# A four-block decoder trunk on one core: the slabs of the down and output projections in halves at the input blocks' place, another order of passes in the products, rotary products on VectorE

## The chip, the cores and the metric

One Trainium2 chip, one of its cores. The metric is the device time of one execution of the whole program in microseconds, as the median of several runs. Before the change three runs took 1076.57, 1079.47 and 1082.0 us; the median is 1079.47 us.

## The reference, cut to what matters

One sequence of 512 tokens, width 1024, all in float32. Two layers, each a token mixer and a feed-forward part with a convolution, both with a root-mean-square norm ahead and a residual behind:

```python
for layer in range(2):
    if layer == 0:
        h = h + short_conv_mixer(rms_norm(h, g), w_in, conv, w_out)   # 1024 -> 3072, conv, gate, -> 1024
    else:
        h = h + mla_attention(rms_norm(h, g), ..., k_nope, v, k_rope) # 8 heads, causal, rotary part of 64
    h = h + conv_ffn(rms_norm(h, g), w_up, conv, w_down)              # 1024 -> 2 x 2816, conv, silu(g) * u, -> 1024
    if layer == 0:
        k_nope, v, k_rope = shared_latent_kv(h, ...)
return rms_norm(h, final_norm)
```

The rotary part of a query is `[x1*cos - x2*sin, x1*sin + x2*cos]`.

## The kernel before

Everything stands transposed in the on-chip memory: features on the 128 partitions, the 512 tokens along the row. A float32 number is split into a rounded high part and a low part (`whi`, `wlo` for weights, names ending in H and L for activations), and a product of two such numbers is three matmul passes: high by high, high by low, low by high. Each matmul loads its own 128x128 weights.

**Weights** come as chunks of eight 128x128 blocks (512 KB) over the SP queue. `Weights.split` (L202, L203) makes the high part on ScalarE and the low part on VectorE. Four chunks are kept ahead.

**Two widths of matmul.** `gemm` (L330) adds up slabs of activations by `mm3` (L311). A slab that is a tuple of three (`halves`, made by `slab`, L429, and by `hg` in `ffn`) is taken in two halves of 256 tokens, six matmuls (L321 to L323); any other slab is taken in three matmuls of 512 (L325 to L327). The up projection runs mostly as seven products of half-size blocks (`product`, L437; a fast scheme with seven products for eight; P1, P2, P6, P5, P7, P4, P3 in that order), 24 matmuls of 256 each (L447 to L449: high by high, high weights by low activations, low weights by high activations). The input blocks of these, `x`, lie in a pool that starts with `pad(xp, 192)` and ends with `pad(xp, 320)` (`start_x`).

**The order of a feed-forward part** is the list `FFN` (L29): two plain column pairs ("p": two gemms of eight slabs, 48 matmuls of 256 each), then column pairs by products ("Q"). From the second "Q" on, four slices of the down projection ("D": `step`, four gemms over the four hidden slabs of a part, 48 matmuls of 512) stand between P7 and P4 of a "Q"; so from one D to the next run P4, P3 and the next pair's P1, P2, P6, P5, P7: seven products, 168 matmuls of 256. There are eight D of this kind in each layer, the last two of them of two slices (24 matmuls). Then follow "p" for columns 20 and 21, the rest of part 3, and the last part ("E"): in layer 0 as gemms, in layer 1 in `down1` (L955), where the weights stream and 128 columns of the hidden slab are the stationary operand. In layer 1 two groups of 16 transposes of `h` ("R") stand between.

The hidden slabs are made in `two` (L533) by `split` (L340), and those of the mixer's output in `gate` (L675), as pairs of 512-wide tiles; they lie where the allocator puts them, in pools on the right side that are that end at a fixed address, in tiles of 2 KB and 4 KB. All weight tiles lie a multiple of 512 bytes from them. The blocks `x` lie 192 bytes past such a multiple, by their pad.

**Norms.** `Norm.sums` multiplies a matrix of ones with the sums of squares (two matmuls of 512, L374 and L375), VectorE makes the diagonals `nd` (L398), and `Norm.spread` (L405) multiplies ones with them (two matmuls of 512). Their tiles `sq` lie in the pool `ap_`, which starts with `pad(ap_, 160)`; they are 320 bytes past a multiple of 512 from the weights (adding up the tiles of the pools). Most of these calls stand in the middle of a gemm; there are six norms of this form.

**Attention** follows the list `ORDER` (L48): v values, r rope, p project, s scores, a attend, t turn (transposes of the softmax), w output. Its start is v0, v1, r0, p0, p1, s0, r1, p2, t0, s1, a0, p3, t1. The framework that builds the program orders each engine's instructions by a plan of its own, so that neighbouring steps may interleave. PSUM has eight banks; `bank()` hands out two groups of four in turn, so the bank of an allocation is that of the eighth before it. In `rope` (L843) two of six products run on GpSimd (L848, L851), four operations on VectorE (L849, L850, L852, L853).

Of the kernel before, what the change touches and what calls it, by code (L numbers as in the profile page):

```python
# [16 lines left out]
P = 128  # L17
# [29 lines left out]

ORDER = [("v", 0), ("v", 1), ("r", 0), ("p", 0), ("p", 1)]  # L48
for _h in range(NH):
    ORDER += [("s", _h)] + ([] if _h else [("r", 1)]) + ([("a", _h - 1)] if _h else [])  # L50
    if _h < 6:
        ORDER += [("p", _h + 2)]
    elif _h == 6:
        ORDER += [("w", 1, 4, 8)]
    else:
        ORDER += [("w", 2, 4, 6)]
    ORDER += [("t", _h)]
    ORDER += {3: [("w", 0, 0, 4)], 4: [("w", 0, 4, 8)], 5: [("w", 1, 0, 4)], 6: [("w", 2, 0, 4)],
              7: [("w", 2, 6, 8)]}.get(_h, [])
ORDER += [("a", 7), ("w", 3, 0, 8)]  # L60
# [201 lines left out]
def trunk(ctx: ExitStack, tc: tile.TileContext, xT, wst, pvec, tabs, sign, gfin, out):  # L262
# [32 lines left out]

    W = Weights(nc, wp, wst)
    pad(ctx.enter_context(tc.tile_pool(name="rp", bufs=1, side="right")), 32)
    pad(ap_, 160)
    sg = ap_.tile([P, 1], F32, name="sg")
    ss = [ap_.tile([P, 8], F32, name=f"ss{tb}") for tb in range(4)]  # L300

# [40 lines left out]
    def split(pool, tag, bufs, src, gain=None):  # L342
# [7 lines left out]
            V.scalar_tensor_tensor(lo, src, gain, hi, op0=ALU.mult, op1=ALU.subtract)  # L350
        return hi, lo

    class Norm:


# [13 lines left out]
        def sums(self, tag=None):  # L369
            hi, lo = (ap_.tile([P, T], F32R, tag="sq", name=nm("na"), bufs=2) for _ in range(2))  # L370
            S.activation(hi, self.acc, AF.Copy)
            V.tensor_tensor(lo, self.acc, hi, op=ALU.subtract)
            ps = bank(tag)
            PE.matmul(ps, ones, hi, start=True, stop=False)  # L374
            PE.matmul(ps, ones, lo, start=False, stop=True)  # L375

            c = ap_.tile([P, 16], F32, tag="nc", name=nm("nc"), bufs=2)
            d = ap_.tile([P, T], F32, tag="sq", name=nm("nd"), bufs=2)
            for b in range(4):
                bs = slice(b * P, b * P + P)  # L380
                V.tensor_tensor_reduce(out=d[:, bs], in0=ps[:, bs], in1=ident, scale=1.0, scalar=0.0,
                                       op0=ALU.mult, op1=ALU.add, accum_out=c[:, b:b + 1])
            v, t, r, e = (c[:, 4 * i:4 * i + 4] for i in range(4))
            V.tensor_scalar(v, v, 1.0 / (self.n * P), EPS, op0=ALU.mult, op1=ALU.add)
            S.activation(t, v, AF.Sqrt)
            V.reciprocal(r, t)
            V.tensor_tensor(t, v, r, op=ALU.mult)
            V.tensor_tensor(t, t, r, op=ALU.mult)
            V.tensor_scalar(t, t, -0.5, 1.5, op0=ALU.mult, op1=ALU.add)
            V.tensor_tensor(r, r, t, op=ALU.mult)  # L390
            rh = ap_.tile([P, 4], F32R, tag="nh", name=nm("nh"), bufs=2)
            S.activation(rh, r, AF.Copy)
            V.tensor_tensor(e, r, rh, op=ALU.subtract)
            self.d, self.r = [], ap_.tile([P, T], F32, tag="rstd", name=nm("rstd"), bufs=2)
            for x in (rh.bitcast(F32), e):
                d = ap_.tile([P, T], F32R, tag="sq", name=nm("nd"), bufs=2)
                for b in range(4):
                    V.tensor_scalar(d[:, b * P:b * P + P], ident, x[:, b:b + 1], None, op0=ALU.mult)  # L398
                self.d.append(d)

        def spread(self, tag=None):

            ps = bank(tag)
            for i, d in enumerate(self.d):
                PE.matmul(ps, ones, d, start=i == 0, stop=i == 1)  # L405
            S.activation(self.r, ps, AF.Copy)

    def conv(pool, tag, src, c, step, bufs=2):
# [27 lines left out]
    def product(p, x, a):  # L436
# [5 lines left out]
        for i in range(KD // 2):  # L442
            ah, al = (t[:, xb * Q:xb * Q + Q] for t in x[i])
            for s in range(2):
                w = slice((s * KD // 2 + i) * P, (s * KD // 2 + i) * P + P)
                o, z = ps[:, s * Q:s * Q + Q], i == KD // 2 - 1
                PE.matmul(o, wh[:, w], ah, start=begins and i == 0 and s == 0, stop=False, skip_group_check=True)  # L447
                PE.matmul(o, wh[:, w], al, start=False, stop=False, skip_group_check=True)  # L448
                PE.matmul(o, wl[:, w], ah, start=False, stop=z, skip_group_check=True)  # L449

    class Out:

# [55 lines left out]
    def ffn(fp, layer, x, rstd, last, late=()):  # L508
# [9 lines left out]
        def tail(j, g, u):  # L518
# [14 lines left out]
            def two():  # L533
                o = conv1(u, 1)
                V.tensor_tensor(o, o, cell[0], op=ALU.mult)
                hid[j] = split(fp, "hid", HID, o)

            cell = []
            pend.extend([one, two])
# [135 lines left out]
    def gate(m, ps, cc):  # L675
        V.tensor_tensor(ps, ps, rstd, op=ALU.mult)
        V.tensor_tensor(ps, ps, cc, op=ALU.mult)
        ys[m] = split(fpp[1], "hid", KD, ps)

    def mix(m, pc, ph, pb):  # L680
        t = room()
# [8 lines left out]
            mm3(ps, W.take(), hg[k], k == 0, k == KD - 1)  # L690
    for k in range(KD):
        norm.add(h[k])
    pss.append([gemm(hg, norm.sums)])
    for i in range(2):
        xsums(x, i, G_MIX, room)
# [74 lines left out]
    if True:  # L770
# [72 lines left out]
        def rope(half):  # L843
# [1 line left out]
            pa, pb = gemm(ql), gemm(ql, None if half else normq.spread)  # L845
            a, b = (scaled(at, "tm", ps, normq.r, 5) for ps in (pa, pb))
            t, u = (at.tile([P, T], F32, tag="tm", name=nm("rp"), bufs=5) for _ in range(2))
            G.tensor_tensor(u, b, sin, op=ALU.mult)  # L848
            V.tensor_tensor(t, a, cos, op=ALU.mult)  # L849
            V.tensor_tensor(a, a, sin, op=ALU.mult)  # L850
            G.tensor_tensor(b, b, cos, op=ALU.mult)  # L851
            V.tensor_tensor(t, t, u, op=ALU.subtract)  # L852
            V.tensor_tensor(a, a, b, op=ALU.add)  # L853
            s1, s2 = split(ao[1], "o", 4, t), split(ao[1], "o", 4, a)
# [81 lines left out]
    if True:  # L936
# [21 lines left out]
        def down1(part, half, hid):  # L958
# [8 lines left out]

            def step(tb, k, i):
                a, z = cuts[tb][i]
                (wh, wl), (ah, al) = (x[:, a:z] for x in ws[k]), (x[:, tb * P:tb * P + P] for x in hid[ks[k]])  # L970
                o = ps[tb][i][:, :z - a]
                PE.matmul(o, ah, wh, start=k == 0, stop=False)  # L972
                PE.matmul(o, ah, wl, start=False, stop=False)  # L973
# [114 lines left out]
```

## Time and profile before

| | us |
|---|---|
| median of three runs | 1079.47 |
| lowest and highest run | 1076.57, 1082.0 |
| the profiled execution | 1076.78 |
| its span, first to last instruction | 1075.0 |
| PE (TensorE matmuls) busy | 1059.3 |
| DVE (VectorE) busy | 919.5 |
| ACT (ScalarE) busy | 561.5 |
| POOL (GpSimd) busy | 46.4 |

The profiled execution is one of its own, 0.2 us above the lowest of the three runs and 2.7 us under their median; 1.8 us of its time lie outside its span. A matmul's duration in the profile (280 ns for 256 columns, 389 ns for 512) has its pipeline in it; successive matmuls overlap, so the time that one costs is read from the starts of successive matmuls in the timeline, over a stretch of known count.

### The profile page before, as it was taken

The numbers are of one execution on the slowest core, as the hardware profiler recorded it, in microseconds if no ns is written. First come the engines' busy times: TensorE is split into PE (matmuls) and PEld (weight loads), VectorE is DVE, ScalarE is ACT, GpSimd is POOL, SyncE is SP. The second block draws the span as 40 slices with busy tenths as digits, with TensorE's granted clock in tenths as the row PEclk, the third lists the DMA queues.
The fourth block names the chain that finished last, engine by engine and source line by source line (L and its number), as shares of the span: only waits on it lengthen the run. The fifth ranks groups of instructions, "written<-read, shape, count | busy, mean of one in ns | idle before, by whom it ended". The sixth has DMA issues, their size and how long they took to land. (4 is left out here: it accounts for less than half of the span.)

```text
span 1075.0 us, 17920 instructions
## 1 busy us (share of the span) xinstructions
PE 1059.3 (99%) x7178; PEld 979.1 (91%) x7178; DVE 919.5 (86%) x1457; ACT 561.5 (52%) x820; POOL 46.4 (4%) x55
## 2 busy tenths in 40 slices
PE   8999999999999999999999899999999999999997
PEld 8999988999999999998887788889999999999986
DVE  7897878799988899986789887899988889989846
ACT  7544455555444455544655554376644445555444
POOL 0000000000000000000001100000000000000000
PEclk9999999999999999999999999999999999999999
DMA  8455433455555465333332412223545545453422
GB/s 269 130 147 141 113 105 109 133 144 141 134 152 124 131 158 137 79 86 97 124 108 82 116 58 60 75 82 119 157 121 153 122 135 157 126 141 72 135 59 79
DMA packets 38115, 129.25 MB, mean 120 GB/s; under 512 B 4752, under 2 KB 5008, under 8 KB 38032
## 3 DMA queue, kind: packets, MB, share of 16 engines
q1 hardware_dynamic: 32240, 107.14, 31.9%
q0 software_dynamic: 5792, 20.98, 11.4%
q8 instruction: 56, 0.92, 0.4%
q14 instruction: 27, 0.22, 0.1%
HBM read 102.67 MB, written 2.10 MB: 97 GB/s over the span
## 5 line engine op out<-in xcount | busy, mean ns | idle before, releaser
L447 PE MATMUL ps<-xH,whi 128*128 128x256 f32 x1120 | 313.6, 280 | 1.4 <-ACT xs L463 1.3
L448 PE MATMUL ps<-xL,whi 128*128 128x256 f32 x1120 | 313.4, 280 | 0.0
L449 PE MATMUL ps<-xH,wlo 128*128 128x256 f32 x1120 | 313.1, 280 | 0.0
L202 ACT ACTIVATE whi<-wraw 128x1024 fp32r<-128x1024 f32 (+1 forms) x130 | 136.5, 1050 | 158.1 <-issue 57.6
L449 PEld LDWEIGHTS ps<-xH,wlo 128*128 128x128 f32 x1120 | 213.8, 191 | 0.0
L447 PEld LDWEIGHTS ps<-xH,whi 128*128 128x128 f32 x1120 | 210.2, 188 | 2.5 <-ACT xs L463 1.5
L448 PEld LDWEIGHTS ps<-xL,whi 128*128 128x128 f32 x1120 | 210.2, 188 | 0.7
L203 DVE TENSOR_TENSOR wlo<-wraw,whi 128x1024 fp32r<-128x1024 f32 (+1 forms) x130 | 158.5, 1219 | 26.9 <-ACT whi L202 26.3
L321 PE MATMUL ps<-xH,whi 128*128 128x256 f32 x512 | 143.4, 281 | 0.5 <-ACT sg L530 0.5
L322 PE MATMUL ps<-xL,whi 128*128 128x256 f32 x512 | 143.2, 280 | 0.0
L326 PE MATMUL ps<-hidL,whi 128*128 128x512 f32 x368 | 143.1, 389 | 0.0
L323 PE MATMUL ps<-xH,wlo 128*128 128x256 f32 x512 | 143.1, 280 | 0.0
L327 PE MATMUL ps<-hidH,wlo 128*128 128x512 f32 x368 | 143.1, 389 | 0.0
L325 PE MATMUL ps<-hidH,whi 128*128 128x512 f32 x368 | 141.9, 389 | 0.0
L202 ACT ACTIVATE whi<-x 128x1024 fp32r<-128x1024 f32 x60 | 63.6, 1060 | 116.5 <-PE ps L326 51.0
L321 PEld LDWEIGHTS ps<-xH,whi 128*128 128x128 f32 x512 | 97.0, 190 | 1.1 <-ACT sg L530 0.7
L323 PEld LDWEIGHTS ps<-xH,wlo 128*128 128x128 f32 x512 | 97.9, 191 | 0.0
L322 PEld LDWEIGHTS ps<-xL,whi 128*128 128x128 f32 x512 | 97.1, 190 | 0.3
L202 ACT ACTIVATE whi<-xs 128x1024 fp32r<-128x1024 f32 x60 | 63.4, 1057 | 64.2 <-PE ps L448 47.1
L327 PEld LDWEIGHTS ps<-hidH,wlo 128*128 128x128 f32 x368 | 69.1, 188 | 14.3
L326 PEld LDWEIGHTS ps<-hidL,whi 128*128 128x128 f32 x368 | 69.1, 188 | 14.2 <-DVE hidL L347 0.2
L325 PEld LDWEIGHTS ps<-hidH,whi 128*128 128x128 f32 x368 | 68.9, 188 | 14.1 <-ACT hidH L346 0.5
(216 smaller groups left out, 1837.7 us busy)
## 6 DMA issues: line engine op xcount, KB each, us to landing
wraw<-wst SPq DMA_DIRECT2D x128, 512.0 KB, 3.7
x<-wst SPq DMA_DIRECT2D x60, 512.0 KB, 4.4
x<-x POOLq DMA_DIRECT2D x20, 512.0 KB, 5.4
xs<-x POOLq DMA_DIRECT2D x20, 512.0 KB, 4.6
h<-xT SPq DMA_DIRECT2D x8, 256.0 KB, 6.2
out<-r SPq DMA_DIRECT2D x8, 256.0 KB, 2.0
qr<-oH SPq DMA_DIRECT2D x16, 64.0 KB, 2.0
qr<-oL SPq DMA_DIRECT2D x16, 64.0 KB, 2.0
```

What stands on the lines that cost most here:

```text
L202: self.nc.scalar.activation(hi, raw, AF.Copy)
L203: self.nc.vector.tensor_tensor(lo, raw, hi, op=ALU.subtract)
L321: PE.matmul(o, wh, p, start=start and b == 0, stop=False, skip_group_check=True)
L322: PE.matmul(o, wh, q, start=False, stop=False, skip_group_check=True)
L323: PE.matmul(o, wl, p, start=False, stop=stop, skip_group_check=True)
L325: PE.matmul(ps, wh, ah, start=start, stop=False)
L326: PE.matmul(ps, wh, al, start=False, stop=False)
L327: PE.matmul(ps, wl, ah, start=False, stop=stop)
L447: PE.matmul(o, wh[:, w], ah, start=begins and i == 0 and s == 0, stop=False, skip_group_check=True)
L448: PE.matmul(o, wh[:, w], al, start=False, stop=False, skip_group_check=True)
L449: PE.matmul(o, wl[:, w], ah, start=False, stop=z, skip_group_check=True)
```

## The change

- The hidden slabs of both feed-forward parts and the mixer's output slabs are marked as halves, so that `mm3` takes them in six matmuls of 256. Their pools get a pad of 320 bytes behind them, which moves the pool's start, and these slabs, down by 320 bytes: that is 192 bytes past a multiple of 512 from the weights, as `x` is.
- The norm's ones-products are made in halves too (`spread2`), and the pad in front of `ap_` shrinks by 128 bytes, with 128 put in behind the `sq` tiles: these then lie 192 bytes past a multiple of 512 from the weights as well.
- `product` takes the low weights second and the low activations third.
- In `rope` the two products on GpSimd go to VectorE.
- In `ORDER` t0 stands ahead of p2 instead of behind it.
- `down1` takes the first two of a hidden slab's three entries; it is as it was otherwise.

```diff
 for _h in range(NH):
-    ORDER += [("s", _h)] + ([] if _h else [("r", 1)]) + ([("a", _h - 1)] if _h else [])
+    ORDER += [("s", _h)] + ([("a", _h - 1)] if _h else [("r", 1), ("t", 0)])
...
-    ORDER += [("t", _h)]
+    ORDER += [("t", _h)] if _h else []
...
-    pad(ap_, 160)
+    pad(ap_, 32)
...
+    def spread2(ps, parts):
+        for b in range(2):
+            for i, d in enumerate(parts):
+                o, d = (t[:, b * Q:b * Q + Q] for t in (ps, d))
+                PE.matmul(o, ones, d, start=i == 0 and b == 0, stop=i == 1, skip_group_check=True)
+
+    padded = []
+
+    def hidden(pool, n, src):
+
+        o = split(pool, "hid", n, src)
+        if pool not in padded:
+            padded.append(pool)
+            pad(pool, 320)
+        return *o, True
...
-            PE.matmul(ps, ones, hi, start=True, stop=False)
-            PE.matmul(ps, ones, lo, start=False, stop=True)
+            spread2(ps, (hi, lo))
...
-            for i, d in enumerate(self.d):
-                PE.matmul(ps, ones, d, start=i == 0, stop=i == 1)
+            spread2(ps, self.d)
...
-                PE.matmul(o, wh[:, w], al, start=False, stop=False, skip_group_check=True)
-                PE.matmul(o, wl[:, w], ah, start=False, stop=z, skip_group_check=True)
+                PE.matmul(o, wl[:, w], ah, start=False, stop=False, skip_group_check=True)
+                PE.matmul(o, wh[:, w], al, start=False, stop=z, skip_group_check=True)
...
-                hid[j] = split(fp, "hid", HID, o)
+                hid[j] = hidden(fp, HID, o)
...
-        ys[m] = split(fpp[1], "hid", KD, ps)
+        ys[m] = hidden(fpp[1], KD, ps)
...
+    pad(ap_, 128)
     pss.append([gemm(hg, norm.sums)])
...
-            G.tensor_tensor(u, b, sin, op=ALU.mult)
+            V.tensor_tensor(u, b, sin, op=ALU.mult)
             V.tensor_tensor(t, a, cos, op=ALU.mult)
             V.tensor_tensor(a, a, sin, op=ALU.mult)
-            G.tensor_tensor(b, b, cos, op=ALU.mult)
+            V.tensor_tensor(b, b, cos, op=ALU.mult)
```

## Rows read from the trace of the kernel before

**Rows 1.** The page: busy time and share of each engine.
```profile
PE 1059.3 (99%) x7178; PEld 979.1 (91%) x7178; DVE 919.5 (86%) x1457; ACT 561.5 (52%) x820; POOL 46.4 (4%) x55
```

**Rows 2.** Waits of PE: releaser, total, times, longest.
```profile
PE ps L876 <- DVE tm L418: 3.2, 1, 3.2
...
PE ps L447 <- ACT xs L463: 1.3, 1, 1.3
PE ps L405 <- DVE nd L398: 0.7, 2, 0.5
```

**Rows 3.** PE's groups by line and shape: count, busy us, mean ns; one of three alike.
```profile
L326 PE MATMUL ps<-hidL,whi 128*128 128x512 f32 x368 | 143.1, 389 | 0.0
```

**Rows 4.** Timeline of PE, start us and us: layer 1, around its first D.
```profile
764.32 0.28 PE L447 MATMUL ps<-xH,whi 128*128 128x256 f32 x1
...
777.92 0.39 PE L325 MATMUL ps<-hidH,whi 128*128 128x512 f32 x1
...
788.82 0.28 PE L447 MATMUL ps<-xH,whi 128*128 128x256 f32 x1
...
808.60 0.39 PE L325 MATMUL ps<-hidH,whi 128*128 128x512 f32 x1
```

**Rows 5.** Timeline of PE around the first norm's two pairs of ones-products.
```profile
29.64 0.28 PE L321 MATMUL ps<-xH,whi 128*128 128x256 f32 x1
...
40.95 0.63 PE L405 MATMUL ps<-nd,ones 128*128 128x512 f32 x2
41.42 0.28 PE L321 MATMUL ps<-xH,whi 128*128 128x256 f32 x1
```

**Rows 6.** Timeline of PE around a wait in layer 0, columns 20 and 21.
```profile
468.52 0.39 PE L321 MATMUL ps<-xH,whi 128*128 128x256 f32 x1 [0.53 <-ACT sg L530]
468.75 0.28 PE L322 MATMUL ps<-xL,whi 128*128 128x256 f32 x1
...
479.53 0.39 PE L325 MATMUL ps<-hidH,whi 128*128 128x512 f32 x1
```

**Rows 7.** Timeline of PE: layer 1 after the transposes; the last 36 of `down1`.
```profile
999.12 0.36 PE L321 MATMUL ps<-xH,whi 128*128 128x256 f32 x1
...
1021.82 0.39 PE L325 MATMUL ps<-hidH,whi 128*128 128x512 f32 x1
...
1063.95 0.28 PE L972 MATMUL ps<-whi,hidH 128*128 128x256 f32 x1
...
1068.14 0.28 PE L974 MATMUL ps<-whi,hidL 128*128 128x256 f32 x1
```

**Rows 8.** Windows: us, busy (count) of PE, PEld, DVE, ACT, POOL, granted clock.
```profile
609.10:613.30 4.20, 4.20 (x11) 3.31 (x12) 4.15 (x19) 1.73 (x5) 0.00 (x0) 0.59 0.45 105
819.50:850.20 30.70, 30.70 (x218) 28.72 (x217) 27.56 (x34) 15.40 (x20) 1.71 (x2) 1.00 0.53 137
217.00:250.00 33.00, 32.82 (x240) 30.82 (x241) 32.99 (x43) 16.22 (x22) 2.59 (x3) 1.00 0.55 138
718.00:778.00 60.00, 59.55 (x512) 59.01 (x511) 59.52 (x106) 40.05 (x55) 1.74 (x2) 1.00 0.45 127
```

**Rows 9.** Timeline of PE, VectorE and GpSimd around the second rope.
```profile
598.49 0.39 PE L325 MATMUL ps<-ckvH,whi 128*128 128x512 f32 x1
599.30 0.47 DVE L888 TENSOR_SCALAR e<-e,st 128x512 f32<-128x512 f32 x1
599.69 2.32 DVE L203 TENSOR_TENSOR wlo<-wraw,whi 128x1024 fp32r<-128x1024 f32 x1
601.00 2.15 POOL L851 TENSOR_TENSOR tm<-tm,ct 128x512 f32<-128x512 f32 x1
601.93 1.77 DVE L849 TENSOR_TENSOR rp<-tm,ct 128x512 f32<-128x512 f32 x1
604.22 0.67 DVE L850 TENSOR_TENSOR tm<-tm,ct 128x512 f32<-128x512 f32 x1
609.09 0.50 PE L876 MATMUL ps<-knH,qsH 128*128 128x512 f32 x1 [3.23 <-DVE tm L418]
```

More of the change, by code (lines that the diff above doesn't have):

```diff
@@ L969, in step @@
                 a, z = cuts[tb][i]
-                (wh, wl), (ah, al) = (x[:, a:z] for x in ws[k]), (x[:, tb * P:tb * P + P] for x in hid[ks[k]])
+                (wh, wl), (ah, al) = (x[:, a:z] for x in ws[k]), (x[:, tb * P:tb * P + P] for x in hid[ks[k]][:2])
                 o = ps[tb][i][:, :z - a]
```

## The prediction

> **What bounds the kernel now.** I read the page first: PE is busy for 1059.3 us, 99% of the span, VectorE for 919.5 [rows 1]. Then PE's waits: the largest is 3.2 us, in the attention, the next behind it in the stream 1.3 [rows 2]. So PE's stream of matmuls is the time, and the question is what one matmul costs in it. The durations in PE's groups do not tell that (389 ns for 512 columns [rows 3]), since matmuls overlap; the starts in the timeline do. In layer 1 five products, 120 matmuls of 256, run from 764.32 to 777.92: 13.60 / 120 = 113.3 ns each. The D behind them, 48 matmuls of 512, takes 10.90 us to 788.82: 227.1 ns each, twice as much. The next seven products, 168 matmuls of the same lines, tiles and shape, take 19.78 us to 808.60: 117.7 ns each [rows 4]. Nothing waits in either stretch. So the 256-wide stream has two speeds, **fast** (113.3) and **slow** (117.7), 4.4 ns apart, and it keeps one until something disturbs it.
>
> What disturbs it can be read. After a run of 512-wide matmuls it starts slow: behind all sixteen D between products, behind the mixer's output projection, behind the attention's. Two ones-products of 512 inside a gemm change it too: after the first norm's sums the 96 matmuls from 29.64 to 40.95 take 117.8 ns, though the stream before was fast; the next pair, at 40.95, brings it back [rows 5]. A wait of PE inside 256-wide work brings it back as well: after the one that ends at 468.52 (0.53 us idle) the 95 matmuls from 468.75 to 479.53 take 113.5 ns [rows 6]. I find no stretch that went from fast to slow without a 512-wide matmul, and no 512-wide run that left it fast, pairs apart.
>
> **The change part by part.**
>
> *Halves in place of 512.* The 368 x 3 = 1104 matmuls of 512 on hidden slabs [rows 3] and the 24 ones-products become pairs of 256. At the fast speed a pair costs 2 x 113.3 = 226.6 ns against 227.1: nothing gained or lost in themselves. At the slow one it costs 235.4, 8.3 ns more. What is gained is that nothing 512-wide is left between the mixer's first gemm and the end of layer 0, nor inside layer 1 up to its transposes, so that the stream should stay fast. The slow matmuls that this reaches, counted by the code: 96 after the first sums; 120 after the output projection, up to the next sums; 120 from the spread to the wait at 217 us; in layer 0, from the first D to the wait at 468 us, 7 x 168 + 48 + 96 = 1320; 80 between sums and spread in layer 1; from its first D to the transposes 7 x 168 + 48 = 1224. That is 2960; x 4.4 ns = **-13.0 us**. This takes for granted that the hidden slabs, at 192 bytes past the weights' place as `x` is, run as `x` runs. The trace bears on the place by one pair of cases: the last 36 matmuls of `down1`, 256 wide and with no such shift, take (1068.14 - 1063.95) / 35 = 119.7 ns [rows 7]. So a 256-wide matmul at the old place would not be fast, and the pads matter.
>
> After the transposes columns 20 and 21 run from 999.12 to 1021.82, 192 matmuls at 118.2 ns [rows 7]. The stream was slow before, and I cannot tell whether transposes keep or set that. If they set it, these stay and the 48 matmuls of 512 behind them cost 48 x 8.3 = **+0.4 us**; if not, another -0.8. I take +0.4.
>
> The Trainium skill, TensorE: Matmul & The Clock Gate, section Back-to-back issue gap, gives a warm matmul its columns by 2.4 GHz and some 2.5 ns besides. By that rule each of the 1128 splits would cost 2.5 ns more, +2.8 us, and the sum would be 1066 us, inside the range below. These rows do not show it: 256 columns take half of what 512 take. I give it 1 in 50, within the forecast's share.
>
> *What is given back.* A faster PE meets others sooner. In layer 1's start VectorE is busy for 59.52 of 60 us, from 217 to 250 for 32.99 of 33 [rows 8]. There PE's waits for `nd` [rows 2] grow by what PE gains ahead of them: 80 x 4.4 = 0.35. From the spread at 201 us PE gains 120 x 4.4 = 0.5 us on VectorE; PE is busy for 32.82 of those 33 us, so that VectorE was still a little ahead: I take 0.15, at worst all 0.5. The wait at 468 us ends by a fixed chain (P3's end, convolution, silu, which frees a bank [rows 6]) that runs beside 96 matmuls: 96 x 4.4 = 0.4 more wait, and in layer 1 the same chain may show, up to 0.4. Together **+1.2**, between 0.3 and 2. Elsewhere VectorE has room: a round of products and D takes 30.7 us and it works 27.56 [rows 8]; the round becomes 30.0.
>
> *Order of passes.* Low weights are wanted one matmul earlier and the chunk's high weights come free one later, 0.11 us. That matters where ScalarE's next split stands ahead of what PE waits for: the wait for `xs` [rows 2], **+0.1**. For the speed of the stream no row shows this order; I take nothing, and carry its bad end as a rival.
>
> *`down1`.* The weights stream there and the hidden slab is stationary. With the slab moved, the two lie 320 bytes apart, as the ones-products did. Those took 0.47 us for two of 512 at 40.95 [rows 5], 235 ns each. 126 matmuls x 8 ns = **+1.0**, between 0 (what they cost now) and 1.1. I take the upper, as the ones are the only row at that distance. The ones-products themselves give 24 x 8 = **-0.2**.
>
> *The attention's start.* Here PE waits 3.23 us until 609.09 for one VectorE operation (L418, p2's query scaling), since s1's last score wants the bank that p2 filled [rows 9]. Then its granted clock is 0.59 (between the levels of 1.2 and 2.4 GHz), and 11 matmuls take 4.22 us [rows 8] against 11 x 0.227 = 2.50: 1.7 us. Wait and clock: 4.95 us. VectorE is late there because GpSimd works beside it: a weight split took 2.32 us and L849 1.77, where L850 took 0.67 alone [rows 9]; that is 1.1 + 1.1. The four products moved add two operations of 0.6 to VectorE in each rope (back to back an operation costs 0.6), 1.2, and take the 2.2 away. And with t0 ahead of p2, s1's banks are those of t0, read by ScalarE and VectorE some 2 us ahead of p2's scaling. Against that, t0 needs s0's softmax, whose last operation ends at 599.30 + 0.47 = 599.77, and PE is through with r1 and starts p2 at 598.49 [rows 9]: a new wait of up to 1.3 us, and PE's a0 stands behind it. So between -4.95 and, if the new waits are as long as the old, +1. I take 4.95 - 1.3 = 3.6: **-3.6 us**. SP's transfers of the rotated queries come a little earlier and nobody on PE waited for them.
>
> *Sum.* -13.0 + 0.4 + 1.2 + 0.1 + 1.0 - 0.2 - 3.6 = -14.1. The profiled execution took 1076.78 us; 1076.8 - 14.1 = 1062.7. It lies 2.7 us under the median of the three runs, whose spread is 5.4; part of that I expect to see in the median after, and round up to **1063.5 us**.
>
> **The rivals.**
>
> *The attention gives nothing.* VectorE has the same work in a new order; the wait may move to t0 or a0 and the clock fall as before. For: in the 4.20 us behind the wait VectorE works 4.15 [rows 8], so it has no room. Against: GpSimd's interference goes. Then 1062.7 + 3.6 = 1066 to 1068 us.
>
> *The stream falls back to slow in part.* Waits shorter than those in the trace, or the first hidden slab of a part that comes late, could set it slow with nothing to lift it until the next long wait. One layer lost: half of 13.0, 6.5, and about 500 split matmuls at 8.3 ns, 4.2: 1062.7 + 10.7 = 1073.
>
> *The split does not do it.* If the products are slow for another reason that sets in after about 20 us of them, halves change nothing there: only the attention, the ones and the small stretches are gained, about 1072 to 1077 us. Against: the five products at 764 us were fast up to the D [rows 4], and so are the mixer's from 49 to 134 us.
>
> *Slower: slow everywhere.* If the new order of passes, or the slabs' place, makes slow the state in which the 256-wide stream settles, the stretches that are fast now (about 1650 matmuls) lose 1650 x 4.4 = 7.2 us, and the split ones 1104 x 8.3 = 9.2. With the attention's gain and `down1`: 1076.8 + 7.2 + 9.2 - 3.6 + 1.0 = 1091. It decides from about 3800 slow matmuls of some 7100 on (3250 are slow now; the other terms pay for 550). Against: the fast state holds in the trace for both kinds of 256-wide work and every weight buffer.
>
> **How the numbers follow.** The forecast has 60 in 100 (1058 to 1067), the attention that gives nothing 15, the partial fall 11, the split that does nothing 7, slow everywhere 7. The range reaches from 1058 (1062.7 less 1.2 if the transposes leave the stream fast, 1.35 for all of the attention's 4.95, 1.0 for `down1`, 0.9 for the waits at their lower end: 1058.2) to 1073, the partial fall. Against the median before, 0.5% is 5.4 us, about what a measurement of this kernel can tell from no change: faster means under 1074. That holds the first two cases and most of the third: 0.83; the rest of it and the split that does nothing make 0.10; slower 0.07.
>
> **What would show it.** Right, if the products between D are at 113.3 ns in both layers, the split D at 226.6 ns a pair, VectorE's share in a round at 92%, and the wait of 3.23 us gone with the granted clock at 1.0 behind it. `down1`'s 512-wide matmuls tell by 227 or 235 whether the distance of 320 costs. Wrong, if a stretch of products behind a split D is at 117.7, or if PE waits for weights or banks in the products by more than 1.2 us in all.

## The result, and the profile after

Four runs of the changed kernel took 1063.84 to 1072.35 us, median 1067.42; four of the kernel before beside them 1076.57 to 1082.0, median 1079.87. The ratio is 0.989, 95% interval [0.9842, 0.9939]. Two more sets of the changed kernel on other occasions had medians of 1069.05 and 1069.23 (ratios 0.9919 [0.9894, 0.9943] and 0.9931 [0.9908, 0.9954]). So the time fell by 8 to 12 us, inside the range; the forecast of 1063.5 is 4 to 6 us too low. The profiled execution took 1072.35 us, the highest of its four, and what follows is read with that in mind.

The page's first row, to be held against [rows 1]: VectorE is as busy as before, GpSimd less by the four products, TensorE's busy time 3 us less.

```profile
PE 1055.9 (99%) x8306; PEld 1018.4 (95%) x8306; DVE 917.2 (86%) x1461; ACT 562.4 (53%) x820; POOL 41.0 (4%) x51
```

PE's waits, against [rows 2]: the 3.2 us in the attention are gone, 1.3 for `xs` became 0.6, 0.5 for `sg` became 1.0. The wait for `hidH` is new. The last line below is from the page's groups: PE's weight loads on hidden slabs have 2.0 us of idle time ahead of them that `hidH` ended.

```profile
PE ps L912 <- DVE e L903: 1.1, 2, 0.6
PE ps L321 <- ACT sg L544: 1.0, 1, 1.0
PE ps L357 <- DVE nd L413: 0.9, 1, 0.9
PE ps L461 <- ACT xs L477: 0.6, 1, 0.6
PE ps L891 <- DVE pt L916: 0.4, 1, 0.4
PE ps L891 <- ACT qsH L346: 0.3, 1, 0.3
PE ps L321 <- ACT hidH L346: 0.2, 1, 0.2
...
L321 PEld LDWEIGHTS ps<-hidH,whi 128*128 128x128 f32 x736 | 137.5, 188 | 2.1 <-ACT hidH L346 2.0
```

PE's timeline in layer 1 (start us, duration us), against [rows 4]. A D is now 96 matmuls of 256 (L321 to L323), products are L461 to L463.

```profile
737.97 0.38 PE L357 MATMUL ps<-nd,ones 128*128 128x256 f32 x1 [0.88 <-DVE nd L413]
...
739.37 0.28 PE L323 MATMUL ps<-xH,wlo 128*128 128x256 f32 x1
...
774.82 0.28 PE L321 MATMUL ps<-hidH,whi 128*128 128x256 f32 x1
...
786.13 0.28 PE L461 MATMUL ps<-xH,whi 128*128 128x256 f32 x1
...
805.91 0.28 PE L321 MATMUL ps<-hidH,whi 128*128 128x256 f32 x1
...
848.26 0.28 PE L461 MATMUL ps<-xH,whi 128*128 128x256 f32 x1
...
867.30 0.28 PE L321 MATMUL ps<-hidH,whi 128*128 128x256 f32 x1
...
878.18 0.28 PE L461 MATMUL ps<-xH,whi 128*128 128x256 f32 x1
```

From 848.26 the 168 matmuls of the products take 19.04 us, 113.3 ns each, and the D behind them 10.88, 226.7 a pair: both as forecast, behind a split D. But from 739.37 to 774.82 the 301 matmuls take 35.45 us, 117.8 each; the D behind them takes 11.31 and the next products, from 786.13 to 805.91, 117.7 each. This slow stretch starts at a wait, the one for `nd`, ahead of which the stream was fast.

It helps to count. I call slow every start-to-start interval of two 256-wide matmuls between 115 and 126 ns, outside the attention, and excess what these take over 113.3 each.

| profiled execution | its time, us | slow matmuls | excess, us | time less excess |
|---|---|---|---|---|
| before | 1076.78 | 3217 | 14.5 | 1062.3 |
| after | 1072.35 | 2249 | 10.1 | 1062.3 |
| after, second set | 1070.92 | 2245 | 10.1 | 1060.8 |
| after, third set | 1074.44 | 3049 | 13.7 | 1060.7 |

The last column stays within 1.6 us, so the state of the stream is nearly all of the difference between these executions. Each of the three profiled executions was the highest of its set; at the medians, 1067 to 1069, the excess would be some 5 to 8 us by the same sum, and 15 to 18 at the medians of before beside them. That is worked out, not read, since those runs have no trace. Nearly all of after's slow matmuls stand in four stretches: 377 from the start to 56 us, 658 from 141 to 218, 855 from 738 to 839, 286 behind the transposes.

### The profile page after: what moved, and what is told of

Its sections match the earlier page's. It is cut to its first block, busy times and chain, and to the rows that moved or that the text cites. A ratio compares the mean times of both kernels' runs of the same rounds, so it can differ in the third digit from the quotient of the medians.

```text
span 1070.6 us, 20133 instructions
## 1 busy us (share of the span) xinstructions
PE 1055.9 (99%) x8306; PEld 1018.4 (95%) x8306; DVE 917.2 (86%) x1461; ACT 562.4 (53%) x820; POOL 41.0 (4%) x51
## 5 line engine op out<-in xcount | busy, mean ns | idle before, releaser
L461 PE MATMUL ps<-xH,whi 128*128 128x256 f32 x1120 | 310.2, 277 | 0.6 <-ACT xs L477 0.6
L463 PE MATMUL ps<-xL,whi 128*128 128x256 f32 x1120 | 310.1, 277 | 0.0
L461 PEld LDWEIGHTS ps<-xH,whi 128*128 128x128 f32 x1120 | 210.3, 188 | 1.0 <-ACT xs L477 0.8
L463 PEld LDWEIGHTS ps<-xL,whi 128*128 128x128 f32 x1120 | 211.0, 188 | 0.0
L462 PEld LDWEIGHTS ps<-xH,wlo 128*128 128x128 f32 x1120 | 210.2, 188 | 0.0
L202 ACT ACTIVATE whi<-wraw 128x1024 fp32r<-128x1024 f32 (+1 forms) x130 | 136.5, 1050 | 139.1 <-issue 64.0
L321 PE MATMUL ps<-hidH,whi 128*128 128x256 f32 x736 | 203.7, 279 | 0.6 <-ACT hidH L346 0.2
L322 PE MATMUL ps<-hidL,whi 128*128 128x256 f32 x736 | 203.3, 278 | 0.1
L323 PE MATMUL ps<-hidH,wlo 128*128 128x256 f32 x736 | 203.0, 277 | 0.0
L321 PE MATMUL ps<-xH,whi 128*128 128x256 f32 x512 | 143.8, 281 | 1.0 <-ACT sg L544 1.0
L323 PE MATMUL ps<-xH,wlo 128*128 128x256 f32 x512 | 143.5, 280 | 0.0
L321 PEld LDWEIGHTS ps<-hidH,whi 128*128 128x128 f32 x736 | 137.5, 188 | 2.1 <-ACT hidH L346 2.0
L323 PEld LDWEIGHTS ps<-hidH,wlo 128*128 128x128 f32 x736 | 138.4, 189 | 0.0
L322 PEld LDWEIGHTS ps<-hidL,whi 128*128 128x128 f32 x736 | 137.8, 188 | 0.3 <-DVE hidL L347 0.3
L202 ACT ACTIVATE whi<-x 128x1024 fp32r<-128x1024 f32 x60 | 63.7, 1061 | 111.5 <-PE ps L322 67.1
L321 PEld LDWEIGHTS ps<-xH,whi 128*128 128x128 f32 x512 | 97.0, 190 | 1.3 <-ACT sg L544 1.2
L323 PEld LDWEIGHTS ps<-xH,wlo 128*128 128x128 f32 x512 | 97.5, 190 | 0.0
L202 ACT ACTIVATE whi<-xs 128x1024 fp32r<-128x1024 f32 x60 | 63.3, 1056 | 42.2 <-PE ps L463 29.0
```

Of the source, the lines that this page charges most:

```text
L202: self.nc.scalar.activation(hi, raw, AF.Copy)
L321: PE.matmul(o, wh, p, start=start and b == 0, stop=False, skip_group_check=True)
L322: PE.matmul(o, wh, q, start=False, stop=False, skip_group_check=True)
L323: PE.matmul(o, wl, p, start=False, stop=stop, skip_group_check=True)
L462: PE.matmul(o, wl[:, w], ah, start=False, stop=False, skip_group_check=True)
L463: PE.matmul(o, wh[:, w], al, start=False, stop=z, skip_group_check=True)
```

## The experiments

The theory of the prediction: 512-wide work sets the stream slow, a wait brings it back, the place of 192 bytes allows the fast speed. Where an expectation speaks of a lottery or of a draw, it means that a restart sets the speed anew, either way.

**TensorE alone.** Groups of eight slabs, 512 and 256 wide, at eight distances between the moving slab and the weights; beside them only ScalarE's copy of each group's result. It computes none of the trunk.

```diff
+    for o in (0, 64, 128, 192, 256, 320, 384, 448):
+        group(o, 8, 512, False, "a")
+        group(o, 8, 256, False, "b")
+        for g in range(5):
+            group(o, 8, 256, False, "c")
+    group(192, 8, 512, False, "a")
+    group(192, 8, 256, True, "b")
+    for g in range(5):
+        group(192, 8, 256, True, "c")
```

`True` puts the low weights second.

> Computes none of the trunk; its output is not the reference's. Only TensorE's stream: for each of eight distances of the moving slabs from the weights (0 to 448 bytes past a multiple of 512, in steps of 64) eight groups of 24 matmuls of 512 columns' worth: one of 512, one of 256 without a gap, five of 256 that each wait for ScalarE to clear the bank; at the end the same at 192 with the low weights second. No DMA and no other engine's work runs beside the matmuls. Theory 'phase' (the speed is set by how weight load and moving stream fall together, the distance decides which speeds exist, and a wait draws one of them anew): at 192 groups at 113.3 and at 117.7 ns both occur among the five behind a wait; other distances have their own one or two speeds, 0 has 119.7. Rival 'neighbours' (slow comes from other engines' reads and writes or from DMA): every distance runs at 113.3. Rival 'width' (my prediction's reading: 512 makes it slow, a wait makes it fast): at 192 the group behind 512 is at 117.7 and all five behind a wait are at 113.3. Order of passes: no difference under all three, unless the last set differs from the one at 192.

PE's timeline: 96 matmuls of 256 at distance 0 (from 21.02), 96 at 192 in the old order of passes (from 141.56), 40 at 448 (from 314.80), then part of a group at 192 in the new order, behind a wait.

```profile
21.02 0.28 PE L301 MATMUL ps<-xh,wh 128*128 128x256 f32 x1
...
32.53 0.40 PE L301 MATMUL ps<-xh,wh 128*128 128x512 f32 x1
...
141.56 0.28 PE L301 MATMUL ps<-xh,wh 128*128 128x256 f32 x1
...
152.87 0.40 PE L301 MATMUL ps<-xh,wh 128*128 128x512 f32 x1
...
314.80 0.28 PE L301 MATMUL ps<-xh,wl 128*128 128x256 f32 x1
...
319.33 0.28 PE L301 MATMUL ps<-xh,wh 128*128 128x256 f32 x1
...
352.73 0.39 PE L301 MATMUL ps<-xh,wh 128*128 128x256 f32 x1 [0.75 <-ACT ev L303]
353.43 0.28 PE L301 MATMUL ps<-xl,wh 128*128 128x256 f32 x1
...
358.07 0.28 PE L301 MATMUL ps<-xh,wl 128*128 128x256 f32 x1
```

(32.53 - 21.02) / 96 = 119.9 ns at distance 0, and 120 at 256; 117.8 at 192, and at 64 and 320; (319.33 - 314.80) / 40 = 113.3 at 448. The 512-wide ones took 226.7 ns at 0, about 233 at 64, 192, 320 and 448. So place repeats with 256 bytes, the two speeds of the 256-wide stream exist without the other engines' work ("neighbours" falls), and distance 192 can hold either: all six groups at 192 in the old order ran at 117.8, while of the groups at 448 the first two were slow and four fast. In the new order all six at 192 were fast, (358.07 - 353.43) / 41 = 113.2.

The two orders are not compared alike in it, though. The framework moved the next distance's 512-wide matmuls, four at a time, in front of each group that was to wait for ScalarE (the rows at 32.53 and 152.87 are such). A wait, 0.75 us, stands only ahead of the last four groups, those in the new order; in the old order the four at 192 stand behind 512-wide matmuls at 256, and the four fast ones at 448 behind such at 192. So this run does not test what a wait does at 192 in the old order, and it shows that 512-wide work at 192 can leave the stream fast.

**The changed kernel with the old order of passes**, run twice.

```diff
-                PE.matmul(o, wl[:, w], ah, start=False, stop=False, skip_group_check=True)
-                PE.matmul(o, wh[:, w], al, start=False, stop=z, skip_group_check=True)
+                PE.matmul(o, wh[:, w], al, start=False, stop=False, skip_group_check=True)
+                PE.matmul(o, wl[:, w], ah, start=False, stop=z, skip_group_check=True)
```

> The changed kernel with the old order of passes in the products (high by high, high by low, low by high). If the order of passes does nothing: products at 113.3 or 117.7 ns as in the changed kernel, the time between 1063 and 1072 us, within 0.5% of it. If the new order helps the stream to stay fast: more stretches at 117.7 than the changed kernel's 2176 slow matmuls, up to +9 us. If it is the new order that makes slow: fewer, down to -9 us.

> The changed kernel with the products' passes in the old order (low activations second, low weights third), again, now beside the changed kernel itself on the same chip. Theory 'with halves the order matters': 1073 to 1077 us, 5 us or more above the changed kernel beside it in nearly every run. Rival 'chance': the speed drawn at a restart has nothing to do with the order; the runs of both lie in one range, about 1065 to 1076, with medians within 2 us.

Medians 1075.32 (ratio to before 0.9982 [0.9962, 1.0001]) and 1074.06 (0.9969 [0.9955, 0.9983]); the changed kernel beside the second took 1069.23. So with halves the order of passes is worth some 5 us, against "I take nothing". One piece can be read at the wait for `xs`: first ScalarE and PE in this kernel, then in the changed one.

```profile
220.18 1.06 ACT L202 ACTIVATE whi<-x 128x1024 fp32r<-128x1024 f32 x1 [1.15 <-PE ps L462]
221.14 0.58 ACT L477 ACTIVATE xs<-ps 128x512 f32<-128x512 f32 x1
...
221.77 0.39 PE L461 MATMUL ps<-xH,whi 128*128 128x256 f32 x1 [1.28 <-ACT xs L477]
```

```profile
218.57 0.60 ACT L477 ACTIVATE xs<-ps 128x512 f32<-128x512 f32 x1 [1.28 <-PE ps L463]
219.06 1.05 ACT L202 ACTIVATE whi<-x 128x1024 fp32r<-128x1024 f32 x1
...
219.22 0.38 PE L461 MATMUL ps<-xH,whi 128*128 128x256 f32 x1 [0.57 <-ACT xs L477]
```

In the new order the chunk's high weights come free one matmul later, and in ScalarE's order, which the framework plans, the split of the next chunk (L202, 1.05 us) now stands behind the operation that PE waits for (L477), where in the old order it stands ahead: 0.7 us gained. The rest, over 4 us, cannot be read from the traces side by side: this kernel's two have 2258 and 2791 slow matmuls, no more than the changed kernel's three. But the first of them was the lowest of its ten runs, and each of the changed kernel's was the highest of its set. By the sum of the table (1071.58 - 10.2 = 1061.4; 1074.51 - 12.5 = 1062.0) this kernel's medians hold an excess of 12 to 14 us, against 5 to 8: an estimate, and enough for all of the rest.

One difference can be counted. Inside a D, PE's waits for a hidden slab left the stream fast in 19 of 19 cases in the changed kernel's three traces, and in 10 of 13 in these two. Behind the other three stand 527, 514 and 379 slow matmuls, 2.3 us of excess in one trace and 3.9 in the other.

**Halves at the old place**: without the pads of 320 bytes, so that the hidden slabs are at distance 0.

```diff
         if pool not in padded:
             padded.append(pool)
-            pad(pool, 320)
+            pass
```

> The changed kernel without the 320-byte pads, so that the hidden slabs lie a multiple of 512 bytes from the weights, still in halves. If the place matters: the 2208 split matmuls run at about 119.7 ns as the last of down1 did, +6.4 ns each, 14 us more than the changed kernel: 1077 to 1085 us; down1's 512-wide matmuls return from 229 to 227 ns, -0.3 us. If it does not: 113.3 or 117.7 there too, 1063 to 1072 us.

1077.87 us in one run. The timeline, D and products in turn:

```profile
778.50 0.28 PE L321 MATMUL ps<-hidH,whi 128*128 128x256 f32 x1
...
790.00 0.29 PE L461 MATMUL ps<-xH,whi 128*128 128x256 f32 x1
...
809.05 0.28 PE L321 MATMUL ps<-hidH,whi 128*128 128x256 f32 x1
...
820.56 0.29 PE L461 MATMUL ps<-xH,whi 128*128 128x256 f32 x1
```

The D takes 119.8 ns a matmul, so the place matters as forecast. The products behind it are fast, 19.05 us for 168, and so behind every D of this trace.

**The attention's part alone**: the kernel before, with the rotary products on VectorE and t0 ahead of p2.

```diff
-            G.tensor_tensor(u, b, sin, op=ALU.mult)
+            V.tensor_tensor(u, b, sin, op=ALU.mult)
-            G.tensor_tensor(b, b, cos, op=ALU.mult)
+            V.tensor_tensor(b, b, cos, op=ALU.mult)
...
-    ORDER += [("s", _h)] + ([] if _h else [("r", 1)]) + ([("a", _h - 1)] if _h else [])
+    ORDER += [("s", _h)] + ([("a", _h - 1)] if _h else [("r", 1), ("t", 0)])
```

> The kernel before with only the rotary products on VectorE and t0 ahead of p2. If the attention's start gained what the trace of the changed kernel shows there (2.85 us between the chunks 146 and 150): 2.5 to 3.5 us less than before, ratio 0.997. If its gain was part of the stream's: no difference, ratio 1.000. The slow stretches stay as before, near 3200 matmuls.

1073.76 us, ratio 0.9966 [0.9952, 0.9979]: 3.4 us. The stream was not as before: the profiled execution, at 1076.81 us the highest of its nine, has 3899 slow matmuls and not some 3200. At the wait for `gx` at 55 us, where the code is still that of before, the stream turned from fast to slow and stayed so for 691 matmuls; before, it stayed fast there. So a wait can set it slow without halves or a new order too.

The score row that waited 3.23 us [rows 9] waits 0.39:

```profile
609.44 0.50 PE L876 MATMUL ps<-knH,qsH 128*128 128x512 f32 x1 [0.39 <-DVE pt L901]
```

From the first matmul on the weights of chunk 146 to that on chunk 150, which holds the attention's start, this kernel and the changed one are both 2.85 us shorter than before. Behind the wait the granted clock of the changed kernel is 1.00 (PE, PEld, DVE, ACT, POOL, then the clock), where it was 0.59 [rows 8]:

```profile
605.00:609.30 4.30, 4.30 (x23) 3.75 (x24) 4.29 (x12) 1.06 (x3) 0.00 (x0) 1.00 0.44 104
```

**The order of passes alone**, in the kernel before; and **attention and order without halves**: the attention's edits above, this one, and low weights second in the plain gemms too.

```diff
-                PE.matmul(o, wh[:, w], al, start=False, stop=False, skip_group_check=True)
-                PE.matmul(o, wl[:, w], ah, start=False, stop=z, skip_group_check=True)
+                PE.matmul(o, wl[:, w], ah, start=False, stop=False, skip_group_check=True)
+                PE.matmul(o, wh[:, w], al, start=False, stop=z, skip_group_check=True)
```

> The kernel before with only the new order of passes in the products; down projection in 512, all else as before. Theory 'entry' (the new order decides into which speed a stretch of products falls when it starts behind a 512-wide run or a wait: fast; the old order falls to slow; either keeps what it has): the seven-product stretches behind each D start fast, at 113.3 ns; some 2400 of the 3219 slow matmuls go, 10 us less than before, 1066 to 1069 us. Rival 'width' (my prediction's reading: 512 wide in front makes them slow whatever the order): 117.7 ns as before, 1076 to 1079 us, no difference.

> The kernel before with the rotary products on VectorE, t0 ahead of p2, and the low weights second in the products and in mm3's halves; hidden slabs in 512 at their old place, ones-products in 512. Theory 'entry': products start fast behind every D without halves, and D stays at 227 ns for 512; 1060 to 1064 us, equal to the kernel with all low weights second or up to 2 us less (no waits on hidden slabs at 113 ns, no shift in down1). Rival 'width': the stretches behind D slow, 1073 us like the attention's part alone.

1078.54 us, ratio 1.001 [0.9993, 1.0028]; and 1074.5, 0.9974 [0.996, 0.9989], what the attention gives alone. In the first, products behind a 512-wide D are as slow as ever, (808.73 - 788.95) / 168 = 117.7 ns:

```profile
788.95 0.28 PE L447 MATMUL ps<-xH,whi 128*128 128x256 f32 x1
...
808.73 0.39 PE L325 MATMUL ps<-hidH,whi 128*128 128x512 f32 x1
```

So the products' own order does not set the speed that they take up behind a 512-wide D, and it gives nothing as long as D is 512 wide.

**The changed kernel with the low weights second in its plain gemms too** (the split gemms of `mm3`).

```diff
-                PE.matmul(o, wh, q, start=False, stop=False, skip_group_check=True)
-                PE.matmul(o, wl, p, start=False, stop=stop, skip_group_check=True)
+                PE.matmul(o, wl, p, start=False, stop=False, skip_group_check=True)
+                PE.matmul(o, wh, q, start=False, stop=stop, skip_group_check=True)
```

> The changed kernel with the low weights second in the halves of mm3 as well, so that all 256-wide work has the new order. Theory 'entry': the stretches that fell to slow in the changed kernel began in mm3's old order (at 11.7, 140.7, 738 and 994 us); now none falls: slow matmuls 2176 to under 400, 8 us less than the changed kernel's profiled run, about 1061 to 1064 us, with less spread between runs. Rival 'lottery' (a wait draws the speed, the order has no part): a few stretches slow, at other places, 1064 to 1072 us.

1070.72 us, 0.9942 [0.9915, 0.9969]: no better. Its trace has 2902 slow matmuls, and stretches that again start at waits (at 140 and 465 us among them).

**The changed kernel again**, twice.

> The changed kernel once more, for comparison on the same chip and for a second look at where it is slow. Under 'entry' and under 'lottery' its slow stretches begin in mm3's halves (at the first gemm, the output projection, the gemm beside the norm) and not always the same ones: 1064 to 1072 us.

> The changed kernel as it is, beside the two others of this set. Theory 'each restart draws a speed anew': its slow stretches stand at other places again than in its two earlier profiles (which agree only from the start to 56 us, from 140 to 218 us and behind the transposes), and its time lies between 1064 and 1072 us. Rival 'fixed by code and addresses': the stretches are those of one of the earlier profiles, and its runs agree within 0.3%.

1069.05 and 1069.23 us. The same stretch of layer 1 in the first of these:

```profile
741.77 0.28 PE L323 MATMUL ps<-xH,wlo 128*128 128x256 f32 x1
...
775.89 0.28 PE L321 MATMUL ps<-hidH,whi 128*128 128x256 f32 x1
...
786.77 0.28 PE L461 MATMUL ps<-xH,whi 128*128 128x256 f32 x1
...
805.81 0.28 PE L321 MATMUL ps<-hidH,whi 128*128 128x256 f32 x1
```

The 301 matmuls take 34.12 us, the D 10.88, the products 19.04: fast, where the first trace of the same kernel was slow up to 839 us. Instead it is slow from 219 to 303 and from 720 to 740; the third is slow at 54 to 141, 229 to 301, 467 to 523 and 741 to 841 us. In the three traces the speed changes only at a wait (the shortest 0.13 us by starts), behind the transposes, behind the attention's 512-wide work, at 10 to 12 us, where 256-wide matmuls go from 213 ns each to one of the two speeds, and once at a ones-product, 1.3 us behind the wait for `nd` (741.3 us in the third). The waits inside a D always left it fast; those for `gx`, `xs`, `sg`, `nd` and in the mixer's output projection went either way.

**One hidden slab in four at distance 0**, the last of each of D's gemms; the others stay at 192.

```diff
+        if at:
+            if pool not in padded:
+                padded.append(pool)
+                pad(pool, 320)
+            return *split(pool, "hidz", z, src), True
+        return *split(pool, "hid", n - z, src), True
...
+                hid[j] = hidden(fp, HID, 2, o, j % 4 == 3)
...
+        ys[m] = hidden(fpp[1], KD, 1, ps, m == KD - 1)
```

> The changed kernel, with one hidden slab in four (the last of each gemm of a D, and the last of the mixer's eight) at distance 0 from the weights and the others at 192 as before. Theory 'last place sets the speed': 256-wide matmuls at distance 0 run at about 120 ns but leave the 256-wide stream behind them fast, as all sixteen D did in the run with every slab at distance 0. Then every run of products behind a D is at 113.3 ns, in both layers, and slow stretches last only from a wait to the next D. Cost: about 500 matmuls at 120 instead of 113.3, +3.3 us; gain: the 1400 to 1500 slow products and split matmuls that the changed kernel's two profiles have behind D's or inside them, 4.4 ns each, -6.4 us: 1064 to 1066 where the changed kernel beside it takes 1067 to 1069. Rival 'the whole D must lie there' or 'chance': products behind some D are at 117.7 although the last 24 of its 96 matmuls were at distance 0; then only the cost shows, 1070 to 1073.

1070.61 us, 0.9936 [0.9918, 0.9954]. The timeline from a stream that a wait had left slow, through its first D (`hidz` is the slab at distance 0):

```profile
740.20 0.28 PE L323 MATMUL ps<-xH,wlo 128*128 128x256 f32 x1
...
775.65 0.28 PE L321 MATMUL ps<-hidH,whi 128*128 128x256 f32 x1
...
777.77 0.28 PE L321 MATMUL ps<-hidzH,whi 128*128 128x256 f32 x1
...
778.49 0.28 PE L321 MATMUL ps<-hidH,whi 128*128 128x256 f32 x1
...
786.78 0.28 PE L462 MATMUL ps<-xH,whi 128*128 128x256 f32 x1
...
805.84 0.28 PE L321 MATMUL ps<-hidH,whi 128*128 128x256 f32 x1
```

Up to 775.65 the 301 matmuls take 117.8 ns each. Six on `hidz` take 0.72 us, and some 0.6 us behind them the stream is fast: the 168 products take 19.06. It is so behind all D of this trace, and in all five places where six or more on `hidz` in a row follow slow matmuls (147, 244, 480, 778 and 1018 us). What was expected of the mechanism holds; the time, 1064 to 1066, does not follow, since each of the 80 gemms with such a slab pays 40 ns for its six (a D from a fast stream takes 11.03 us for 10.88), 3.2 us, and the mixer drew slow in the profiled run (733 matmuls).

**One low tile of the input blocks at distance 0**, so that a lone matmul there comes every twelve.

```diff
+    def tiles_x(xp, mid):
+        n = KD // 2
+        x = [[xp.tile([P, 8 * 256], F32R, tag="x" + t, name=nm("x" + t), bufs=n - (t == "L"))
+              for t in ("HL" if i < n - 1 else "H")] for i in range(n)]
+        mid()
+        x[-1].append(xp.tile([P, 8 * 256], F32R, tag="xz", name=nm("xz"), bufs=1))
+        return x
...
-        pad(xp, 320)
-        return x
+        return tiles_x(xp, lambda: pad(xp, 320))
```

> The changed kernel with one of the eight tiles that hold the input blocks, the low part of the last pair, at distance 0 from the weights instead of 192; it is the moving operand of 408 of the 4896 matmuls on input blocks, two in each product, always one at a time among matmuls at 192. The hidden slabs stay at 192. Theory 'any 256-wide matmul at distance 0 makes the stream fast': every product and plain gemm pulls the stream back to 113.3 ns within one product (24 matmuls), so slow stretches no longer last; the 2200 to 3000 slow matmuls of the changed kernel's profiles fall under 500 (-8 to -11 us), and the 408 cost 7 to 10 ns more each (+3 to +4): 1062 to 1066 us. Rival 'it takes several in a row' (each slab that did it in the last set was six matmuls in a row): slow stretches go through whole products as before, and only the cost shows: 1071 to 1074 us.

1075.81 us, 0.9989 [0.9981, 0.9998]. Two passes of a product's last block, in a fast stream and in a slow one:

```profile
102.13 0.28 PE L468 MATMUL ps<-xz,whi 128*128 128x256 f32 x1
...
102.97 0.28 PE L466 MATMUL ps<-xH,whi 128*128 128x256 f32 x1
...
881.94 0.28 PE L468 MATMUL ps<-xz,whi 128*128 128x256 f32 x1
...
882.77 0.28 PE L466 MATMUL ps<-xH,whi 128*128 128x256 f32 x1
```

Two of each seven intervals begin at a matmul on `xz`. The seven take 0.84 us where 7 x 113.3 = 0.79 were due, and 0.83 where 7 x 117.7 = 0.82 were. So a lone matmul at distance 0 costs a fast stream 20 to 25 ns and leaves it fast, costs a slow one nothing and leaves it slow. The rival held: it takes several in a row. Its 1071 to 1074 us were missed, since a lone one had been priced at 7 to 10 ns.

## Why the prediction was right in sign and range, and where it failed

**What bounds the kernel, the two speeds, the halves.** Right: between the profiled executions the whole gain outside the attention and the `xs` wait is in start-to-start times of 256-wide matmuls. Where the stream is fast, split D and products have the forecast 226.7 a pair and 113.3. Without halves there is no such gain, whatever the order of passes. The rule by which the Trainium skill (TensorE: Matmul & The Clock Gate, section Back-to-back issue gap) would charge each split 2.5 ns, there given for an isolated matmul, is not borne out in this stream: 96 matmuls of 256 in 10.88 us are 48 of 512 at 226.7 ns. Two parts were not tried alone: the ones-products in halves at their new place, and the slabs at distance 192 but 512 wide, which in the small kernel cost 6 to 7 ns a matmul more and left the stream fast four times.

**The step that failed** is in the reading of what disturbs the stream: "A wait of PE inside 256-wide work brings it back". A wait can set the speed either way. The trace of before had four waits of over 0.3 us by starts in the products and plain gemms, three from slow to fast and one that left the stream fast, which looked like a rule; after's has one at 139.7 us and one at 737 that went from fast to slow, and the same waits, those inside a D apart, end differently from run to run. The prediction's own sign of being wrong is met: the products behind the first split D of layer 1 took 117.7 ns. So the term of -13.0, which counted every stretch set slow by 512-wide work as saved, was too large: between the profiled executions it measured -4.4 (an excess of 10.1 us left of 14.5), and at the medians, by the same sum, some -6 to -12. The start is part of it: the 377 matmuls up to 56 us were fast in the third set's trace, and in before but for 96 behind the first sums; in the other two of the changed kernel they were slow. This is the rival "The stream falls back to slow in part", with its price between that of the forecast and that rival's 10.7, and its reason in waits of many kinds; those for a late slab inside a D, which it names, left the stream fast every time. The medians, 1067.4 to 1069.2, lie above the forecast's own case (1058 to 1067) and within the range because that was stretched to this rival's 1073.

**Order of passes.** "I take nothing" for the speed was wrong with halves: 1074.06 against 1069.23 in one set. The price of +0.1 at `xs` had the wrong sign, -0.7: I saw that high weights come free later, and not that the plan of ScalarE would then put the wanted operation first. Halves without the order (with the attention's part) give 0.9969 to 0.9982, no more than the attention alone; the order without halves nothing; both together some 5 us more. That the order makes more restarts fall fast fits the excess worked out for the medians (12 to 14 us in the old order, 5 to 8 in the new) and the waits inside a D (10 of 13 fast against 19 of 19). The small kernel does not settle it, since its groups in the two orders stand behind different things, and how the order would do it stays open.

**Given back.** The +0.4 at columns 20 and 21 came as forecast (`sg`, 0.5 to 1.0). Not in the sum were seven waits of 0.28 to 0.51 us inside a D, by starts 2.6 us in all. One of them ends at 899.50: ScalarE around it in the trace after, then in the same D of before:

```profile
897.42 0.60 ACT L477 ACTIVATE xs<-ps 128x512 f32<-128x512 f32 x1 [1.66 <-PE ps L463]
897.91 1.05 ACT L202 ACTIVATE whi<-xs 128x1024 fp32r<-128x1024 f32 x1
898.86 0.59 ACT L346 ACTIVATE hidH<-ps 128x512 fp32r<-128x512 f32 x1
```

```profile
900.73 1.06 ACT L202 ACTIVATE whi<-xs 128x1024 fp32r<-128x1024 f32 x1 [1.76 <-PE ps L448]
901.70 0.58 ACT L346 ACTIVATE hidH<-ps 128x512 fp32r<-128x512 f32 x1
902.17 0.59 ACT L463 ACTIVATE xs<-ps 128x512 f32<-128x512 f32 x1
```

After, the D starts at 897.22 and its fourth slab is ready 2.2 us later; before, it starts at 900.65 and the slab is ready after 1.6. The weight split (L202) stands ahead of the slab (L346) in both. New is that the copy of `xs` stands ahead of the split, the same swap that gained 0.7 us at the wait for `xs`. It is not the swap alone: with halves and the old order of passes the copy stands behind again, and PE waits there too, 0.40 us by starts, for the slab's low part from VectorE. "Elsewhere VectorE has room" was right in its share (27.37 us of a round of 29.92, 91%, against a forecast 92%), but what changed at this wait is the order on ScalarE, not a share.

**The attention.** The mechanism was right: wait gone, clock at full. Its -3.6 measured -2.85 between the marks; the new waits (two of 0.6 for `e`, 0.4 for `pt`, and 0.3 for `qsH`, L891) together are 1.8, where I took 1.3. The rival by which it gives nothing fell.

**`down1`.** +1.0 was too much. Its 126 wide matmuls take 229.7 ns each at distance 320, where the same sum gave 227.9 before: +0.23, and its last 36 take 113.3 to 117.8 in place of 119.7. The ones-products at that distance (235), where the ones are the fixed operand, were a poor stand-in; why the two differ is not shown.

**Behind the transposes** the 192 matmuls take 118.2 ns in all three traces, as taken. "Slow everywhere" fell: 4847 intervals of the trace after are fast.

The terms that are not about the stream nearly cancel: the attention -2.85 and `xs` -0.7 against 2.6 for the hidden slabs, 0.4 for `sg` and 0.2 for `down1`, which is why the time less excess is the same before and after.

## What to carry to other kernels

Read a matmul's price from successive starts, in stretches, and compare several traces of one kernel before calling a stretch's speed a rule: here the same code ran at either of two speeds, and one trace showed only one way in which a wait can turn it. When an engine gets faster, list for each step what stands ahead of the awaited operation on every engine, before and after, and not only on the engine that is busiest. A gain that needs two edits together shows in neither alone, so undo each from the full version as well as trying it from the old one.

## What the runs showed of the hardware

- With the same instructions, tiles and addresses a stream of 256-wide matmuls at distance 192 holds 113.3 or 117.7 ns each for up to 855 matmuls, and changes only at a wait, the transposes, or work of another width or place (once at a ones-product). The same wait can end either way; those for a slab inside a D, in the new order of passes, ended fast 19 times of 19.
- The distance between the moving operand and the weights counts by its remainder to 256 bytes: 119.9 ns at 0 and 256 (226.7 for 512 columns), 117.8 or 113.3 at 192 and 448 (about 233 for 512 columns). A 512-wide run at 0 or 256 left the stream behind it slow (all sixteen D of before among them), four 512-wide ones at 192 left it fast (four times), a 256-wide run at 0 of six or more left it fast; a lone matmul at 0 changed nothing and cost up to 25 ns.
- Why a restart falls one way or the other was not found.
